# Which products in parts of the array stand together: whole sets of scores, and values behind the next scores

## The chip, the cores and the metric

The kernel runs on one core of a Trainium2 chip. The metric is the device time of one execution in microseconds (us). An execution with the hardware profiler attached gives the trace; its own time stands beside the times of the runs without it.

## The reference

One step of a hybrid encoder layer, for 512 frames of a prompt and for 8 samples with 16 new frames each (640 tokens of width 1024, all float32). Cut to what matters:

```
x += 0.5 * SwiGLU_1(norm(x))                  # width 2816
h  = norm(x);  z = h @ w_in_mix               # one projection for both mixers and the gates
x += (g_ret * Br_ret(retention) + g_fox * Br_fox(fox)) @ w_out
x += 0.5 * SwiGLU_2(norm(x))
x += (p @ W_ple) * sigmoid(norm(x) @ W_ple_gate)

fox, prompt : 8 heads of 64; causal softmax(q k^T / 8 + c_i - c_j) v, in blocks of 128 queries
fox, sample : 16 queries against 1024 cached keys and values and 16 new ones, per sample and head
retention   : 4 heads, key width 128, value width 256; 512 prompt frames in chunks, and per
              sample one chunk of 16 on a given state; the new states are outputs
```

The new keys, values, forget values and retention states are outputs too.

## The kernel before

The work is written as one long program, and a planner (the framework's scheduler, with a timeline of its own) puts each engine's instructions in an order; among what is ready by that timeline it takes what stands earlier in the program. On the chip each engine then runs its own list in that order.

Stages: the first SwiGLU; then, from about 470 to 1020 us of the span, the mixer; then the output projections, the second SwiGLU and the embedding. In the mixer a stream of *units* (`run_units`, line 845: projections of 256 columns, their weights split in two parts for exactness) is the bulk of TensorE's work. `fill(us)` (line 1582) writes so many us of units into the program, and between two fills the steps of the attention and of the retention are written: sixteen sets of the prompt's attention (lines 1604 to 1611), eight samples of eight steps (1617 to 1621), four heads of retention (1641 to 1651). `defer(us, f)` (line 760) writes `f` later, when the program's estimated clock has moved on by so much; `pump` writes what is due. `after(inst, name, why)` (line 209) orders one instruction behind another in the planner's list; on the chip it is no wait. `load` (line 212) issues from SyncE's queue.

TensorE's array has 128 rows and 128 columns. A product with 64 rows of weights or fewer, or 64 columns or fewer, takes a part of the array, and several stand side by side in it. Four kinds of them are touched here; each float32 product shows as two weight loads and two products in the trace (the pick products as one):

- *Prompt scores* (`prompt_scores`, line 1164): for head pair `pr` and query block `i` two heads in 64 rows each, one bank a head: first a product that brings the bias (`pick`, 40 rows), then queries times keys.
- *Prompt values* (`values`, line 1202): two heads in 64 columns each, for `i + 1` key blocks, into one bank; written by `defer(1.5, ...)` after the second head's weights have been flipped and copied.
- *Sample scores and values* (`Sample`, line 1221): four pairs of heads in 32 columns each. A sample has two halves (`s`) of 512 cached frames: a half's scores are four products of 512 columns, written 1.8 us after the copy of the fourth pair's transposed keys. The values are 36 products of 128 columns, written in three parts, each after the flip of its part of the weights (`flip`, line 1298).
- *Retention, samples* (`values_s`, line 1419, four lanes of 32 columns; `states`, line 1464, four lanes of 32 rows into four banks).

In the order of the lanes the kernel before always begins with the first, and the `after` lines tie the first lane behind the work that the others need:

```
if r == 0:
    for _, made in four[2:]:
        after(m, made.ins.name, "the four pairs of heads side by side in the array")
```

Buffers that this touches: six banks of the tag `pa`, eight tiles of the tag `att` (transposed keys, softmax weights, flipped weights), and four buffers of 1 MB (`kv`) in which two halves of keys and two of values pass. `Sample.loads` (line 1233) writes the loads in the order: next keys' first half, both halves of values, next keys' second half.

Of the kernel before, what the change touches and what calls it, by code (L numbers as in the profile page):

```python
# [19 lines left out]
P = 128  # L20
# [111 lines left out]
def kernel(  # L132
# [1028 lines left out]

    pair_bank, pair_pts = [None], [None, None]

    def prompt_scores(hu, pr, i):

        n, both = (i + 1) * P, pair()
        for h2, ps in enumerate(both):
            head, rows = hu * 4 + 2 * pr + h2, slice(h2 * FD, h2 * FD + 40)
            last = mm(ps[:, :n], pick[rows, head:head + 1].to_broadcast([40, P]), c_row[0][rows, :n], True, False, skip_group_check=True)
        for h2, ps in enumerate(both):  # L1170
            rows = slice(h2 * FD, (h2 + 1) * FD)
            m = mm(ps[:, :n], qk_out[hu][rows, 0, pr, i * P:n], qk_out[hu][rows, 1, pr, :n], False, True, skip_group_check=True)
            if h2 == 0:
                after(m, last.ins.name, "the pair of heads side by side in the array")
        for h2, ps in enumerate(both):
            prompt_softmax(hu, 2 * pr + h2, i, n, ps)

    def prompt_softmax(hu, h, i, n, ps):
# [12 lines left out]
        def flipped():  # L1191
            pt = bank()
            for j in range(i + 1):
                transpose(pt[:, j * P:(j + 1) * P], pe[:, j * P:(j + 1) * P])
            pts = att()
            done = nc.scalar.copy(pts[:, :n], pt[:, :n])
            pair_pts[h % 2] = (pts, done)
            if h % 2 == 1:
                both = list(pair_pts)
                defer(1.5, lambda: values(both))  # L1200

        def values(both):
            pr = h // 2
# [3 lines left out]
            for j in range(i + 1):  # L1207
                for h2 in range(2):
                    m = mm(po[h2 * FD:(h2 + 1) * FD, i * P:n], v_p[hu][j][:, (2 * pr + h2) * FD:(2 * pr + h2 + 1) * FD],
                           both[h2][0][:, j * P:(j + 1) * P], j == 0, j == i, skip_group_check=True)  # L1210
                    if j == 0 and h2 == 0:
                        after(m, both[1][1].ins.name, "the pair of heads side by side in the array")
            if i == 3:
# [7 lines left out]
    class Sample:  # L1221
# [20 lines left out]
        def step(self, n):  # L1242
# [15 lines left out]
            kts = att()  # L1258
            if pr % 2 == 0:
                done = nc.vector.tensor_copy(kts, pt)  # L1260
            else:
                done = nc.scalar.copy(kts, pt)
# [4 lines left out]
            if pr == 3:  # L1267
                four = self.kts

                def scores():  # L1270

                    for r, (kt, _) in enumerate(four):
                        m = mm(self.ps[s][r * 32:(r + 1) * 32, :], qof(r, self.b), kt, False, True, skip_group_check=True)
                        if r == 0:
                            for _, made in four[2:]:
                                after(m, made.ins.name, "the four pairs of heads side by side in the array")
                    nc.vector.tensor_reduce(self.mx[:, s:s + 1], self.ps[s], axis=AX.X, op=ALU.max)
                    if s == 1:
                        self.softmax()
# [18 lines left out]
        def flip(self, s):  # L1298
            if s == 0:
                nc.vector.tensor_reduce(self.rc, self.sums, axis=AX.X, op=ALU.add)  # L1300
                nc.vector.reciprocal(self.rc, self.rc)
                self.po = bank()
            n = 4 if s < 2 else 1
# [6 lines left out]
            else:  # L1310
                nc.scalar.copy(pts[:, :n * P], pt[:, :n * P])
            defer(1.5, lambda: self.values(s, pts, n))

        def values(self, s, pts, n):
            for j in range(n):
                for pr in range(4):
                    rhs = (self.v[4 * s + j] if s < 2 else vnew)[:, pr * P:(pr + 1) * P]
                    mm(self.po[pr * 32:(pr + 1) * 32, :P], pts[:, j * P + pr * 32:j * P + (pr + 1) * 32], rhs,
                       s == 0 and j == 0, s == 2, skip_group_check=True)
            if s == 2:  # L1320
                om = tmp([P, P])
                nc.vector.scalar_tensor_tensor(om, self.po[:, :P], self.rc, cs["bd"], op0=ALU.mult, op1=ALU.mult)
                defer(1.5, lambda: self.fold(om))

# [8 lines left out]
    class Retention:  # L1333
# [130 lines left out]
        def states(self):  # L1464
# [3 lines left out]
            for j in range(2):  # L1468
                for r in range(NB // 2):
                    rows = slice(r * 32, (r + 1) * 32)  # L1470
# [133 lines left out]
    for hu in (0, 1):  # L1604
# [3 lines left out]
        for pr in range(2):  # L1608
            for i in range(4):
                prompt_scores(hu, pr, i)  # L1610
                fill(2 * (FILL_P0 if hu == 0 else FILL_P1))
    samples = [Sample(b) for b in range(NB)]
    defer(0.0, sample_new)
# [27 lines left out]
    for hd, r in enumerate(heads):  # L1641
        for step in (
            lambda: r.rotate(0), lambda: r.rotate(1), lambda: (r.flip(), heads[hd + 1].first_loads() if hd + 1 < RH else None),
            lambda: r.scores(), lambda: r.scores_s(),
            lambda: (r.states_p(), heads[hd + 1].loads() if hd + 1 < RH else None),
            lambda: r.values(0), lambda: r.values(1), lambda: r.values_s(),
            lambda: (r.sizes(), until(("rg", hd)), r.gates()),
            lambda: (r.states(), heads[hd + 1].more_loads() if hd + 1 < RH else None), lambda: r.finish(),
        ):
# [131 lines left out]
```

## Time and profile before

| | |
|---|---|
| median of three runs | 1638.36 us (1637.53 to 1638.69) |
| the profiled execution | 1636.49 us, span 1634.5 us |
| TensorE busy | 1624.8 us, 11979 products |
| VectorE, ScalarE, GpSimd busy | 1164.5, 733.1, 94.5 us |
| memory traffic | 242.88 MB, mean 149 GB/s |
| a 1 MB load of cached values, issue to landing | 6.7 us (median) |
| a 1 MB load of cached keys, issue to landing | 6.2 us (median) |

How to read the rows: PE is TensorE's product, PEld its weight load (in the trace both have an entry), DVE VectorE, ACT ScalarE, POOL GpSimd, SPq SyncE's queue. L205 is a line of the kernel; many products have the line of the helper `mm`, so they are told apart by the tiles (`pa<-kv,att`: written and read) and by their form: `128*32` is a weight load of 128 rows and 32 columns. In brackets stands how long the engine was idle before and what ended that; "issue" is no other engine.

### The profile page before, as it was taken

How to read it: one execution, taken by the hardware profiler on the slowest of the kernel's cores; microseconds unless marked ns; L12 is line 12 of the kernel's file. 1: busy time of each engine (PE TensorE's matmuls, PEld its weight loads, DVE VectorE, ACT ScalarE, POOL GpSimd, SP SyncE). 2: the span in 40 equal slices, each digit the busy share in tenths (PEclk: the TensorE clock that was granted, in tenths of full speed). 3: DMA queues.
4: the chain of work that ended last, by engine and by line, in shares of the span. 5: the costliest groups of instructions: out<-in, count | busy, mean ns of one | idle time of the engine just before them, and what ended most of it. 6: DMA issues, size and time to landing. Idle time of an engine off the chain costs nothing.

```text
span 1634.5 us, 30303 instructions
## 1 busy us (share of the span) xinstructions
PE 1624.8 (99%) x11979; PEld 1555.4 (95%) x11979; DVE 1164.5 (71%) x2472; ACT 733.1 (45%) x1536; POOL 94.5 (6%) x172
## 2 busy tenths in 40 slices
PE   9999999999999999999999999999999999999999
PEld 8999999999999888888789898999999999999998
DVE  7985786577776755767688996557885787578663
ACT  7552354244455444444334454435553355235432
POOL 0000000000011111000000011001000000000000
PEclk9999999999999999999999999999999999999999
DMA  7244233433533234566776477534334323332531
GB/s 247 78 144 142 86 94 118 150 94 108 186 107 104 99 113 138 210 254 249 284 248 209 159 258 261 177 101 163 98 100 142 126 82 132 135 118 88 173 122 46
DMA packets 205566, 242.88 MB, mean 149 GB/s; under 512 B 10176, under 2 KB 175984, under 8 KB 201328
## 3 DMA queue, kind: packets, MB, share of 16 engines
q1 hardware_dynamic: 193824, 200.07, 37.0%
q0 software_dynamic: 11392, 40.79, 6.3%
q8 instruction: 94, 1.54, 0.4%
q14 instruction: 48, 0.39, 0.1%
q10 hardware_dynamic: 208, 0.08, 0.0%
HBM read 194.89 MB, written 46.03 MB: 147 GB/s over the span
## 4 chain that ended last, share of the span: by engine, by line
PE 97%; ACT 1%; DVE 1%; DMA 1%; issue 0%; SPq 0%; DVEq 0%
PE pa L205 74%; PE pg L205 19%; PE pa L228 4%; ACT tmp L533 0%; DMA raw<-in_ffn_w_in_dram 0%; PE pg L228 0%; ACT wh L282 0%; DMA kv<-in_x_prompt_dram 0%; DVE kv L1474 0%; ACT blk L361 0%; DVE wl L283 0%; DVE raw L424 0%; DVE tmp L573 0%; ACT blk L353 0%; DVE raw L420 0%
## 5 line engine op out<-in xcount | busy, mean ns | idle before, releaser
L282 ACT CAST wh<-raw 128x512 fp32r<-128x512 f32 (+1 forms) x525 | 315.8, 613 | 493.2 <-PE pa L205 315.0
L205 PE MATMUL pa<-blk,wh 128*128 128x320 f32 x2344 | 509.0, 310 | 1.9 <-ACT wh L282 0.9
L283 DVE TENSOR_TENSOR wl<-raw,wh 128x512 fp32r<-128x512 f32 (+1 forms) x525 | 352.0, 679 | 95.2 <-ACT wh L282 91.5
L205 PEld LDWEIGHTS pa<-blk,wh 128*128 128x128 f32 x2344 | 386.8, 188 | 8.5 <-ACT wh L282 2.3
L205 PE MATMUL pa<-blk,wl 128*128 128x320 f32 x1172 | 343.0, 309 | 0.0
L205 PE MATMUL pa<-kv,wh 128*128 128x320 f32 x1344 | 251.6, 308 | 0.0
L205 PEld LDWEIGHTS pa<-blk,wl 128*128 128x128 f32 x1172 | 215.4, 188 | 0.1
L205 PEld LDWEIGHTS pa<-kv,wh 128*128 128x128 f32 x1344 | 210.7, 188 | 0.0
L205 PE MATMUL pg<-blk,wh 128*128 128x320 f32 x768 | 176.6, 316 | 1.1 <-DVE blk L833 1.1
L205 PE MATMUL pa<-blk,blk 128*128 128x320 f32 (+2 forms) x1064 | 168.7, 304 | 0.0
L205 PE MATMUL pa<-kv,wl 128*128 128x320 f32 x672 | 154.6, 308 | 0.0
L205 PEld LDWEIGHTS pa<-blk,blk 128*128 128x128 f32 (+1 forms) x1064 | 151.8, 183 | 2.0 <-PE pa L205 1.2
L205 PE MATMUL pg<-wh,blk 128*128 128x256 f32 x768 | 148.4, 286 | 0.0
L205 PEld LDWEIGHTS pg<-blk,wh 128*128 128x128 f32 x768 | 127.4, 188 | 8.0 <-issue 4.1
L205 PEld LDWEIGHTS pg<-wh,blk 128*128 128x128 f32 x768 | 120.8, 188 | 6.4 <-issue 5.2
L205 PE MATMUL pg<-blk,wl 128*128 128x320 f32 x384 | 118.8, 309 | 0.0
L205 PEld LDWEIGHTS pa<-kv,wl 128*128 128x128 f32 x672 | 112.6, 188 | 0.0
L205 PE MATMUL pg<-wl,blk 128*128 128x256 f32 x384 | 108.4, 283 | 0.0
L205 PE MATMUL pa<-wh,blk 128*128 128x256 f32 (+1 forms) x432 | 82.3, 285 | 0.0
L283 DVE TENSOR_TENSOR blk<-raw,blk 128x512 fp32r<-128x512 f32 x82 | 56.3, 689 | 34.8 <-ACT blk L282 23.6
L282 ACT CAST blk<-raw 128x512 fp32r<-128x512 f32 x82 | 50.6, 621 | 51.8 <-DMA raw<-in_ffn_w_in_dram 41.5
L205 PEld LDWEIGHTS pg<-wl,blk 128*128 128x128 f32 x384 | 72.2, 188 | 1.6 <-issue 1.1
(287 smaller groups left out, 2225.4 us busy)
## 6 DMA issues: line engine op xcount, KB each, us to landing
raw<-in_ffn_w_in_dram SPq DMA_DIRECT2D x86, 512.0 KB, 4.7
raw<-in_w_in_mix_dram SPq DMA_DIRECT2D x25, 1024.0 KB, 5.6
raw<-in_ffn_w_out_dram SPq DMA_DIRECT2D x16, 1024.0 KB, 5.1
kv<-in_cache_fox_k_dram SPq DMA_DIRECT2D x16, 1024.0 KB, 6.2
kv<-in_cache_fox_v_dram SPq DMA_DIRECT2D x16, 1024.0 KB, 6.7
blk<-xd SPq DMA_DIRECT2D x48, 320.0 KB, 5.4
xd<-blk POOLq DMA_DIRECT2D x40, 320.0 KB, 3.0
zdram<-blk POOLq DMA_DIRECT2D x24, 320.0 KB, 4.0
```

Source lines behind the costliest of these rows:

```text
L205: i = nc.tensor.matmul(out, lhsT, rhs, start=start, stop=stop, **kw)
L228: tick(nc.tensor.transpose(out, in_, ident[: in_.shape[0], : in_.shape[0]]), 0.11)
L282: nc.scalar.copy(hi, src)
L283: nc.vector.tensor_tensor(lo, src, hi, op=ALU.subtract)
```

## The change

1. Prompt scores: the lanes run second head first, for the bias and for the scores; the `after` hangs on the second head's score.
2. Prompt values: no longer written by `defer(1.5, ...)`. They go into a list `values_due`, and the next set of scores, of the prompt or of a sample, writes them directly behind its last product, with an `after` on it. The second head goes first, behind the first head's copy. What is left after the prompt is written 7 us later.
3. Sample scores: fourth pair first, ordered behind the copies of the other three. The copies of pairs 0 and 1 are on VectorE and those of 2 and 3 on ScalarE (before: 0 and 2, 1 and 3).
4. Sample values: the three parts are collected, and all 36 products are written in one run behind the next sample's first scores (the last sample's 1.5 us after its last flip). Their bank is taken then.
5. Retention: `states` loops over its four banks from the last, and is written in the same step as `values_s`, two steps earlier than before; the next head's state load stays in its step.

```diff
--- before.py
+++ after.py
@@ -1159,19 +1159,21 @@
         nc.vector.tensor_reduce(mnew, snew, axis=AX.X, op=ALU.max)
 
 
-    pair_bank, pair_pts = [None], [None, None]
+    pair_bank, pair_pts, values_due = [None], [None, None], []
 
     def prompt_scores(hu, pr, i):
 
         n, both = (i + 1) * P, pair()
-        for h2, ps in enumerate(both):
+        for h2, ps in ((1, both[1]), (0, both[0])):
             head, rows = hu * 4 + 2 * pr + h2, slice(h2 * FD, h2 * FD + 40)
             last = mm(ps[:, :n], pick[rows, head:head + 1].to_broadcast([40, P]), c_row[0][rows, :n], True, False, skip_group_check=True)
-        for h2, ps in enumerate(both):
+        for h2, ps in ((1, both[1]), (0, both[0])):
             rows = slice(h2 * FD, (h2 + 1) * FD)
             m = mm(ps[:, :n], qk_out[hu][rows, 0, pr, i * P:n], qk_out[hu][rows, 1, pr, :n], False, True, skip_group_check=True)
-            if h2 == 0:
+            if h2 == 1:
                 after(m, last.ins.name, "the pair of heads side by side in the array")
+        while values_due:
+            values_due.pop(0)(m)
         for h2, ps in enumerate(both):
             prompt_softmax(hu, 2 * pr + h2, i, n, ps)
 
@@ -1197,19 +1199,21 @@
             pair_pts[h % 2] = (pts, done)
             if h % 2 == 1:
                 both = list(pair_pts)
-                defer(1.5, lambda: values(both))
-
-        def values(both):
+                values_due.append(lambda behind: values(both, behind))
+
+        def values(both, behind):
             pr = h // 2
             if i == 0:
                 pair_bank[0] = bank()
             po = pair_bank[0]
             for j in range(i + 1):
-                for h2 in range(2):
+                for h2 in (1, 0):
                     m = mm(po[h2 * FD:(h2 + 1) * FD, i * P:n], v_p[hu][j][:, (2 * pr + h2) * FD:(2 * pr + h2 + 1) * FD],
                            both[h2][0][:, j * P:(j + 1) * P], j == 0, j == i, skip_group_check=True)
-                    if j == 0 and h2 == 0:
-                        after(m, both[1][1].ins.name, "the pair of heads side by side in the array")
+                    if j == 0 and h2 == 1:
+                        after(m, both[0][1].ins.name, "the pair of heads side by side in the array")
+                        if behind is not None:
+                            after(m, behind.ins.name, "with the other products in parts of the array")
             if i == 3:
                 f = blk([P, S])
                 nc.vector.tensor_copy(f, po)
@@ -1256,7 +1260,7 @@
             for j in range(4):
                 transpose(pt[:, j * P:(j + 1) * P], self.k[4 * s + j][:, pr * P:(pr + 1) * P])
             kts = att()
-            if pr % 2 == 0:
+            if pr < 2:
                 done = nc.vector.tensor_copy(kts, pt)
             else:
                 done = nc.scalar.copy(kts, pt)
@@ -1269,11 +1273,14 @@
 
                 def scores():
 
-                    for r, (kt, _) in enumerate(four):
+                    for r in (3, 2, 1, 0):
+                        kt = four[r][0]
                         m = mm(self.ps[s][r * 32:(r + 1) * 32, :], qof(r, self.b), kt, False, True, skip_group_check=True)
-                        if r == 0:
-                            for _, made in four[2:]:
+                        if r == 3:
+                            for _, made in four[:3]:
                                 after(m, made.ins.name, "the four pairs of heads side by side in the array")
+                    while values_due:
+                        values_due.pop(0)(m)
                     nc.vector.tensor_reduce(self.mx[:, s:s + 1], self.ps[s], axis=AX.X, op=ALU.max)
                     if s == 1:
                         self.softmax()
@@ -1299,7 +1306,7 @@
             if s == 0:
                 nc.vector.tensor_reduce(self.rc, self.sums, axis=AX.X, op=ALU.add)
                 nc.vector.reciprocal(self.rc, self.rc)
-                self.po = bank()
+                self.pts = []
             n = 4 if s < 2 else 1
             pt = bank()
             for j in range(n):
@@ -1309,18 +1316,24 @@
                 nc.vector.tensor_copy(pts[:, :n * P], pt[:, :n * P])
             else:
                 nc.scalar.copy(pts[:, :n * P], pt[:, :n * P])
-            defer(1.5, lambda: self.values(s, pts, n))
-
-        def values(self, s, pts, n):
-            for j in range(n):
+            self.pts += [pts[:, j * P:(j + 1) * P] for j in range(n)]
+            if s == 2:
+                if self.b + 1 < NB:
+                    values_due.append(self.values)
+                else:
+                    defer(1.5, lambda: self.values(None))
+
+        def values(self, behind):
+            po = bank()
+            for j, pt in enumerate(self.pts):
                 for pr in range(4):
-                    rhs = (self.v[4 * s + j] if s < 2 else vnew)[:, pr * P:(pr + 1) * P]
-                    mm(self.po[pr * 32:(pr + 1) * 32, :P], pts[:, j * P + pr * 32:j * P + (pr + 1) * 32], rhs,
-                       s == 0 and j == 0, s == 2, skip_group_check=True)
-            if s == 2:
-                om = tmp([P, P])
-                nc.vector.scalar_tensor_tensor(om, self.po[:, :P], self.rc, cs["bd"], op0=ALU.mult, op1=ALU.mult)
-                defer(1.5, lambda: self.fold(om))
+                    rhs = (self.v[j] if j < 8 else vnew)[:, pr * P:(pr + 1) * P]
+                    m = mm(po[pr * 32:(pr + 1) * 32, :P], pt[:, pr * 32:(pr + 1) * 32], rhs, j == 0, j == 8, skip_group_check=True)
+                    if j == 0 and pr == 0 and behind is not None:
+                        after(m, behind.ins.name, "with the other products in parts of the array")
+            om = tmp([P, P])
+            nc.vector.scalar_tensor_tensor(om, po[:, :P], self.rc, cs["bd"], op0=ALU.mult, op1=ALU.mult)
+            defer(1.5, lambda: self.fold(om))
 
         def fold(self, om):
             pf = bank()
@@ -1466,7 +1479,7 @@
             hd = self.hd
             pss = [bank() for _ in range(NB // 2)]
             for j in range(2):
-                for r in range(NB // 2):
+                for r in reversed(range(NB // 2)):
                     rows = slice(r * 32, (r + 1) * 32)
                     mm(pss[r][:, j * DV:(j + 1) * DV], self.kb[rows, j, :], self.vs[4][rows, :], True, True)
             for r in range(NB // 2):
@@ -1609,6 +1622,7 @@
             for i in range(4):
                 prompt_scores(hu, pr, i)
                 fill(2 * (FILL_P0 if hu == 0 else FILL_P1))
+    defer(7.0, lambda: [values_due.pop(0)(None) for _ in range(len(values_due))])
     samples = [Sample(b) for b in range(NB)]
     defer(0.0, sample_new)
     samples[0].load(samples[0].k, cache_k)
@@ -1643,9 +1657,9 @@
             lambda: r.rotate(0), lambda: r.rotate(1), lambda: (r.flip(), heads[hd + 1].first_loads() if hd + 1 < RH else None),
             lambda: r.scores(), lambda: r.scores_s(),
             lambda: (r.states_p(), heads[hd + 1].loads() if hd + 1 < RH else None),
-            lambda: r.values(0), lambda: r.values(1), lambda: r.values_s(),
+            lambda: r.values(0), lambda: r.values(1), lambda: (r.values_s(), r.states()),
             lambda: (r.sizes(), until(("rg", hd)), r.gates()),
-            lambda: (r.states(), heads[hd + 1].more_loads() if hd + 1 < RH else None), lambda: r.finish(),
+            lambda: heads[hd + 1].more_loads() if hd + 1 < RH else None, lambda: r.finish(),
         ):
             step()
             fill(FILL_R)
```

## Rows read from the trace of the kernel before

**Rows 1.** The page: busy time of the engines, and the chain that ended last

```profile
PE 1624.8 (99%) x11979; PEld 1555.4 (95%) x11979; DVE 1164.5 (71%) x2472; ACT 733.1 (45%) x1536; POOL 94.5 (6%) x172
...
PE 97%; ACT 1%; DVE 1%; DMA 1%; issue 0%; SPq 0%; DVEq 0%
```

**Rows 2.** Waits of TensorE's products, 500 to 1030 us: who for whom, total, times, longest

```profile
PE pg L205 <- DVE blk L833: 1.1, 1, 1.1
PE pa L228 <- DVE att L1188: 0.3, 1, 0.3
```

**Rows 3.** Waits of the weight loads, 500 to 1030 us

```profile
PEld pa L205 <- issue: 15.5, 70, 0.8
PEld pa L228 <- issue: 11.6, 29, 0.8
```

**Rows 4.** Timeline of the weight loads, prompt values: start, us, engine, count

```profile
639.85 0.31 PEld L205 LDWEIGHTS pg<-wh,blk 128*128 128x128 f32 x2
640.29 0.19 PEld L205 LDWEIGHTS pa<-att,kv 128*64 128x64 f32 x2
640.65 0.19 PEld L205 LDWEIGHTS pg<-wl,blk 128*128 128x128 f32 x1 [0.17 <-issue]
...
641.08 0.85 PEld L205 LDWEIGHTS pa<-att,kv 128*64 128x64 f32 x14
642.10 0.19 PEld L205 LDWEIGHTS pg<-wh,blk 128*128 128x128 f32 x1 [0.17 <-issue]
```

**Rows 5.** The same timeline, prompt values with scores, and a set of scores alone

```profile
585.33 0.85 PEld L205 LDWEIGHTS pa<-att,kv 128*64 128x64 f32 x14
...
586.87 0.19 PEld L205 LDWEIGHTS pg<-wh,blk 128*128 128x128 f32 x1
...
620.96 0.19 PEld L205 LDWEIGHTS pa<-att,pick 40*128 40x128 f32 x2
...
621.98 0.19 PEld L205 LDWEIGHTS pg<-wh,blk 128*128 128x128 f32 x1 [0.54 <-issue]
```

**Rows 6.** The same timeline, sample scores and values in three stretches of time

```profile
688.00 0.16 PEld L205 LDWEIGHTS pa<-blk,tmp 128*32 128x32 f32 x8 [0.15 <-issue]
688.36 0.19 PEld L205 LDWEIGHTS pg<-blk,wl 128*128 128x128 f32 x1 [0.20 <-issue]
688.70 0.16 PEld L205 LDWEIGHTS pa<-att,blk 128*32 128x32 f32 x8 [0.15 <-issue]
689.70 0.30 PEld L205 LDWEIGHTS pa<-sm,tmp 128*128 128x128 f32 x2 [0.84 <-DVE tmp L1322]
...
719.05 0.14 PEld L205 LDWEIGHTS pa<-att,blk 128*32 128x32 f32 x4 [0.19 <-issue]
720.03 0.42 PEld L228 LDWEIGHTS pa<-sm,kv 128*128 128x128 f32 x4 [0.84 <-DVE blk L827]
...
802.60 0.81 PEld L205 LDWEIGHTS pa<-kv,att 128*32 128x32 f32 x32
...
804.68 0.19 PEld L205 LDWEIGHTS pa<-blk,blk 128*128 128x128 f32 x1 [0.20 <-PE pa L205]
```

**Rows 7.** Groups by line and form on VectorE, 650 to 850 us: the keys' copies

```profile
L1260 DVE COPY att<-pa 128x512 f32<-128x512 f32 x31 | 21.3, 688 | 7.7 <-PE pa L228 7.4
```

**Rows 8.** Timeline of SyncE's queue: a pair of value loads

```profile
709.83 1.60 SPq L214 DMA_DIRECT2D kv<-in_cache_fox_v_dram  x2
```

**Rows 9.** Timeline of the weight loads, retention: state products

```profile
925.38 0.31 PEld L205 LDWEIGHTS pa<-kv,tmp 32*128 32x128 f32 x8 [0.19 <-PE pa L205]
926.02 0.30 PEld L205 LDWEIGHTS pg<-blk,wh 128*128 128x128 f32 x2 [0.33 <-issue]
926.28 0.19 PEld L205 LDWEIGHTS pg<-blk,wl 128*128 128x128 f32 x1
```

**Rows 10.** Busy time by stage: PE, PEld, DVE, ACT, POOL, clock, DMA

```profile
650.00:840.00 190.00, 189.99 (x1683) 157.76 (x1681) 129.91 (x277) 81.58 (x183) 13.98 (x23) 1.00 0.67 245
840.00:960.00 120.00, 118.88 (x868) 110.70 (x867) 112.39 (x242) 51.50 (x114) 9.06 (x15) 1.00 0.58 199
```

## The prediction

> **What bounds the kernel now.** I read the page first: TensorE is busy for 99% of the span, and the chain that ended last lies on it for 97% [rows 1]. So the end is set by how long TensorE's own stream lasts. Then I read the waits in the attention and retention (500 to 1030 us): TensorE's products waited for another engine for 1.4 us in all [rows 2]. The same view for the weight loads tells something else: 27.1 us of idle in 99 places ahead of its loads for one kind of bank, put down to "issue", that is, to no other engine [rows 3]. The timeline shows what these are [rows 4]. Whole-array loads come 0.117 us apart; the second of the pair at 639.85 starts at 639.97, so the next was due at 640.08. It comes at 640.29, because it is the first for half of the array's columns; and it is 640.65 before a whole-array load comes again. Two loads for a part of the array cost 0.20 + 0.36 = 0.56 us of the stream. The fourteen left over from the same set cost 0.20 + (642.10 - 641.08) = 1.22 us, for what a whole set of sixteen at 615.23 also takes. What goes ahead alone is paid in full. I call such an unbroken run of part-array products a stretch, and its cost the time from the last whole-array load ahead of it to the first behind it, less one pitch. That is the currency of this change.
>
> Added up over the timeline: the prompt's attention has 39 stretches of 39.1 us together (first at 513.78, last at 641.08), the samples' 40 of 52.0 us (655.87 to 843.36), the retention 18 of 19.0 us (864.26 to 1007.57). PE time alone is at stake, 110 us of it.
>
> **The change part by part.** The number of products stays. What changes is in how many stretches they stand.
>
> *Prompt scores.* A whole set costs 1.22 us for three key blocks [rows 5], and 0.27 more or less a block: 0.69, 0.95, 1.22, 1.49 us, together 4.35, four times. Before, five of the sixteen sets are broken, either because the first head's pick product goes ahead while the second head's bank is still taken, or because one head's scores go alone. The new order begins with the head whose bank comes last, so that the other is ready when it starts.
>
> *Prompt values.* A set costs 0.57, 0.79, 1.00, 1.22 us for one to four blocks, 3.58 together, four times. Six of sixteen are broken like the one above: the first head's product waits only until the second head's copy has been placed, not until it is done. The new order starts with the head that is copied last. Both kinds whole and apart: 4 x (4.35 + 3.58) = 31.7 us. Now the values also stand directly behind scores. Such a joint is there once before: fourteen value loads with a one-block set cost 0.20 + (586.87 - 585.33) = 1.74 us [rows 5], apart 1.22 + 0.69 = 1.91. A joint of two splits, rows then columns, saves 0.17; fifteen save 2.5. With 1.1 us for the samples' new-frame scores, which stay: 30.3. **Saved: 39.1 - 30.3 = 8.8 us.**
>
> *Samples.* A whole set of scores (eight loads) costs 0.20 + (689.70 - 688.70) = 1.20 us, and half a set, four loads, 0.20 + (720.03 - 719.05) = 1.18 [rows 6]: four lanes run in the time of two. Nine of sixteen sets stand in two pieces and two more are interleaved lane by lane with values, since the copies of the last pairs of keys (0.69 us on VectorE [rows 7]) end after the first lane has started. The change starts with the last pair. The 36 value products of a sample come in three runs of 32, 32 and 8 loads, mostly apart; eight alone cost 0.19 + (688.36 - 688.00) = 0.55 us. Behind scores they pay no entry of their own, since both split columns in four: forty value loads and eight score loads stand together once, for 0.20 + (804.68 - 802.60) = 2.28 us [rows 6], so a value load adds (2.28 - 1.20) / 40 = 0.027. Seventy-two with the scores: 2.28 + 32 x 0.027 = 3.14. Seven samples at 3.14 + 1.20, the first one's 2 x 1.20, the last one's values alone 0.55 + 64 x 0.027 = 2.28: 35.1 us. **Saved: 52.0 - 35.1 = 16.9 us.**
>
> Here a rule speaks against the change, and a row answers it. The row: eight loads of a column-split set are through in 0.16 us [rows 6]. The Trainium skill, "TensorE: Matmul & The Clock Gate", section "Part 3: Packing small matmuls", says that a weight load overlaps running products only where its row group differs. All lanes of the samples' scores and values read rows 0 to 127; by that rule whole sets would gain nothing, some 10 of the 16.9 us would not come, and the sum below would end near 1624. The trace disagrees with it at these shapes, so I keep the 16.9.
>
> *What the samples' move drags along.* Values now run after the next sample's first scores, so the two value buffers, two transposed blocks and a bank are given back then. The value loads stand in SyncE's queue ahead of later key and weight loads. Before, the pair at 709.83 [rows 8] is issued right as values and next scores pass (708.7 to 711.9); afterwards at the same place or up to 3 us later. Landing takes 6.7 us (the profile's table), and these values are multiplied from 731.5 on: 13 us of cover; a key or weight load behind them has at least as long. The bank is now taken for 3 us instead of some ten. The later multiply, fold and store have no reader before the branch projection. The swapped copies leave 16 a sample-half on either engine: nothing.
>
> *Retention.* The state products (16 loads, rows split in four) move two steps up, behind the samples' values. With them move four VectorE updates (0.68 us each) ahead of the root and scaling, and a store on GpSimd's queue; the next state's load stays where it was. Eight loads cost 0.20 + (926.02 - 925.38) = 0.84 us [rows 9]; a second eight adds 0.43 (twelve, at 972.07, cost 1.28), so a whole set 1.27. Before, they stand in two to four pieces a head, their banks coming free one by one; the reversed order waits for the last bank. Values cost 1.23 whole, but in three heads one lane goes ahead for 0.95, and nothing in the diff ends that; I keep it. One place where columns then rows join saves 0.24. So 4 x (1.23 + 1.27 - 0.24) + 3 x 0.95 = 11.9. **Saved: 19.0 - 11.9 = 7.1 us.**
>
> *Taken off.* Behind a stretch the stream makes up 0.03 us (two loads in 0.26 us [rows 9], where the usual pitch of these makes 0.29): 97 stretches become about 43, so 1.6. From 840 to 960 us VectorE is busy 112.4 of 120 us [rows 10] (the same rows show the clock granted in full), and TensorE cannot run far ahead of what it prepares; I take half of the retention's gain away, 3.5 (bounds 0 and 7.1). Sets will still be cut where an earlier matrix product becomes ready between two lanes; before, about one in ten is cut without its own operand being late. Four more pieces at 0.8: 3.2 (bounds 0 and 12).
>
> Sum: 8.8 + 16.9 + 7.1 - 1.6 - 3.5 - 3.2 = 24.5 us. The profiled execution took 1636.5, so 1612.0; the median of the runs is 1.9 us above it, so **1614**. What bounds it afterwards is the same stream. Without the last two discounts it is 1607; with the upper ends of both, 1626.
>
> **Rivals.** *The sets stay in pieces.* The order on TensorE is made by the planner by its own times, and products from earlier in the program go first. For it: sets are cut now although all their operands are there (values of the retention, scores at 513.78 to 518.03). Against it: most prompt sets after 560 us, with the old order, are already whole. If half of the gain goes this way: 1638.4 - 12 = 1626.
>
> *The wait for the last operand moves onto TensorE (slower).* Each set now begins with its latest operand. The planner's times are not the chip's; where it takes a copy to be done that is not, TensorE stands, in order, with everything behind it. Price: up to one copy, 0.69 us [rows 7], in each of about 64 sets: 44 us, which gives 1638 - 24 + 44 = 1658. It decides from a mean of 24/64 = 0.38 us a set. Against it: before, after the same kind of copies, such waits sum to a few us in 500 us [rows 2, 3], at similar distances.
>
> *VectorE becomes the bound.* With 16 us less of TensorE from 650 to 840, VectorE's 129.9 in 190 us [rows 10] become 75%; only 840 to 960 has no room. If all that the retention and the last two samples gain is given back there: 1638 - 24 + 7 = 1621, inside the range.
>
> **How the numbers follow.** Forecast 0.70 (its own range 1607 to 1624), sets in pieces 0.15, the rule on column splits 0.01, VectorE 0.04 on top of what is taken off, the wait for the last operand 0.07, and 0.03 for pieces and waits that cancel. A measurement of this kernel tells about 0.2% (3.3 us) from no change. Faster 0.88, same 0.05, slower 0.07. The range 1605 to 1631 leaves out the slower case and the worst of the pieces.
>
> **What would show it.** Right: between 500 and 1030 us the weight loads' "issue" idle falls from the 99 places of [rows 3] to under 60; score loads come in eights with 72 value loads in the same stretch; state loads stand in sixteens; TensorE's busy share stays 99%. Wrong: score loads in fours and sixes; new waits of the first load of a set for a copy or a bank; TensorE idle for VectorE after 840 us; value loads landing behind their use.

## The result, and the profile after

Time after: 1622.67 us median of 5 runs (1621.34 to 1622.75), against 1638.36 us (1637.53 to 1638.73): ratio 0.9903, 95% interval 0.9888 to 0.9917. The kernel is 15.7 us faster; 24.4 were forecast (1614), and the time lies inside the range of 1605 to 1631. The profiled execution took 1622.67 us; that of before was 1.9 us under its median, so the two profiles are 13.8 us apart.

The page after shows the same bound as [rows 1]:

```profile
PE 1609.3 (99%) x11979; PEld 1557.3 (96%) x11979; DVE 1164.4 (72%) x2472; ACT 731.5 (45%) x1536; POOL 94.5 (6%) x172
...
PE 96%; DMA 2%; DVE 1%; ACT 1%; issue 0%; SPq 0%; DVEq 0%
```

The weight loads' waits from 500 to 1030 us answer [rows 3]. Columns: who for whom, total us, times, longest.

```profile
PEld pa L205 <- issue: 14.0, 57, 0.8
PEld pa L228 <- issue: 8.7, 16, 0.8
```

The 99 places have become 73, where under 60 were expected. Added up over the timeline in the prediction's own currency, the stretches became:

| part | before: count, us | forecast whole, us | after: count, us |
|---|---|---|---|
| prompt | 39, 39.1 | 30.3 | 35, 36.3 |
| samples | 40, 52.0 | 35.1 | 18, 35.8 |
| retention | 18, 19.0 | 11.9 | 15, 18.0 |
| sum | 97, 110.1 | 77.3 | 68, 90.1 |

So 20.0 us of stretches went, 16.2 of them from the samples. The timeline of the weight loads shows the samples as they were forecast, in place of [rows 6]: eight score loads, 64 of the values and 8 of the new frame's values, until a whole-array load comes again.

```profile
683.08 0.16 PEld L205 LDWEIGHTS pa<-att,blk 128*32 128x32 f32 x8 [0.19 <-issue]
683.54 0.13 PEld L205 LDWEIGHTS pa<-kv,att 128*32 128x32 f32 x4 [0.30 <-issue]
683.97 1.66 PEld L205 LDWEIGHTS pa<-kv,att 128*32 128x32 f32 x60 [0.30 <-issue]
685.60 0.24 PEld L205 LDWEIGHTS pa<-blk,tmp 128*32 128x32 f32 x8
686.04 0.42 PEld L228 LDWEIGHTS pa<-sm,kv 128*128 128x128 f32 x4 [0.20 <-PE pa L205]
```

Entry, loads and exit take 0.19 + (686.04 - 683.08) = 3.15 us; 3.14 was forecast. Six such runs stand in the trace, where seven were forecast: one sample's 72 value loads (786.62 us) stand apart from the scores, for 2.30 us. All sixteen sets of scores come in eights; those that stand alone cost 1.19 to 1.23 us.

The prompt and the retention look otherwise. The same timeline, in order: the prompt's first sets, still lane by lane as before; a single pick product ahead of its set; and, in the retention, two state loads that join the values, the other fourteen 4 us later (compare [rows 9]).

```profile
525.38 0.29 PEld L205 LDWEIGHTS pa<-kv 64*128 64x128 f32 x2
526.01 0.19 PEld L205 LDWEIGHTS pg<-wh,blk 128*128 128x128 f32 x1 [0.33 <-ACT att L1037]
...
613.57 0.18 PEld L205 LDWEIGHTS pa<-att,pick 40*128 40x128 f32 x1
613.88 0.19 PEld L205 LDWEIGHTS pg<-wh,blk 128*128 128x128 f32 x1
614.19 0.18 PEld L205 LDWEIGHTS pa<-att,pick 40*128 40x128 f32 x1
614.20 0.41 PEld L205 LDWEIGHTS pa<-kv 64*128 64x128 f32 x4
...
907.82 0.29 PEld L205 LDWEIGHTS pa<-kv,tmp 32*128 32x128 f32 x2 [0.41 <-issue]
...
912.16 0.74 PEld L205 LDWEIGHTS pa<-kv,tmp 32*128 32x128 f32 x14 [0.20 <-PE pg L205]
```

New is a wait of TensorE at the change from samples to retention. TensorE's products there; the last number is the idle time ahead of the row:

```profile
828.86 0.31 PE L205 MATMUL pg<-blk,wl 128*128 128x320 f32 x1
831.75 0.57 PE L205 MATMUL pa<-sm,tmp 128*128 128x64 f32 x2 [2.59 <-DVE tmp L1335]
...
833.04 0.73 PE L205 MATMUL pa<-blk,wh 128*128 128x320 f32 x2
833.57 0.47 PE L205 MATMUL pa<-blk,wl 128*128 128x320 f32 x1
833.84 0.73 PE L205 MATMUL pa<-blk,wh 128*128 128x320 f32 x2
...
835.39 0.46 PE L205 MATMUL pg<-blk,wh 128*128 128x320 f32 x2
835.69 0.31 PE L205 MATMUL pg<-blk,wl 128*128 128x320 f32 x1
835.83 0.46 PE L205 MATMUL pg<-blk,wh 128*128 128x320 f32 x2
```

Behind the wait three products take 833.84 - 833.04 = 0.80 us, from 835.39 on 0.44: the granted clock is at its half level, 1.2 GHz, from 831.9 to 835.3. The twelve products from 832.09 to 835.39 take 3.30 us where 12 x 0.147 = 1.76 would do: 1.5 us. VectorE's timeline shows who is waited for:

```profile
825.19 0.69 DVE L424 TENSOR_TENSOR raw<-raw 128x512 f32<-128x512 f32 x1
829.88 1.56 DVE L1374 TENSOR_TENSOR kv<-kv,blk 128x640 f32<-128x640 f32 x2 [4.00 <-DMA blk<-in_c_rope_dram]
831.36 0.34 DVE L1335 SCALAR_TENSOR_TENSOR tmp<-pa,ty,sm 128x128 f32<-128x128 f32 x1
```

The last sample's masked sums (L1335) stand in VectorE's queue behind the retention's first rotation (L1374), and this one waits 4.00 us for the rope tables, which SyncE issues here:

```profile
813.95 4.23 SPq L214 DMA_DIRECT2D kv<-zdram  x6
...
822.05 1.16 SPq L214 DMA_DIRECT2D blk<-in_c_rope_dram  x2
```

Before, the first table was issued at 830.86 us and the rotation (line 1361 there) began at 840.30:

```profile
830.86 0.43 SPq L214 DMA_DIRECT2D blk<-in_c_rope_dram  x1
...
840.30 0.82 DVE L1361 TENSOR_TENSOR kv<-kv,blk 128x640 f32<-128x640 f32 x1
```

After, the two are 7.8 us apart, and for 4.0 of them VectorE stands ready. The last sample's scores run 20 us earlier (811.9 instead of 832 us), the tables are issued only 9 us earlier.

### The profile page after: what moved, and what is told of

The parts are those of the page before. It is cut to its first block, busy times and chain, and to the rows that moved or that the text cites. A ratio compares the mean times of both kernels' runs of the same rounds, so it can differ in the third digit from the quotient of the medians.

```text
span 1620.9 us, 30289 instructions
## 1 busy us (share of the span) xinstructions
PE 1609.3 (99%) x11979; PEld 1557.3 (96%) x11979; DVE 1164.4 (72%) x2472; ACT 731.5 (45%) x1536; POOL 94.5 (6%) x172
## 4 chain that ended last, share of the span: by engine, by line
PE 96%; DMA 2%; DVE 1%; ACT 1%; issue 0%; SPq 0%; DVEq 0%
PE pa L205 74%; PE pg L205 18%; PE pa L228 4%; DMA kv<-zdram 1%; DMA blk<-in_c_rope_dram 0%; DMA raw<-in_ffn_w_in_dram 0%; ACT tmp L533 0%; PE pg L228 0%; DVE wl L283 0%; ACT wh L282 0%; DMA kv<-in_x_prompt_dram 0%; SPq L214 0%; DVE kv L1487 0%; ACT blk L361 0%; DVE blk L1473 0%
```

## The experiments

The runs of the kernel before beside these had medians of 1637.86 (17 runs), 1637.89 (15) and 1638.09 us (7).

**The three parts by themselves.** Each kernel is the one before with one part of the diff: `s_alone` the samples, `p_alone` the prompt, `r_alone` the retention. `s_order` has the samples' new order of lanes and copies alone, the values staying in three runs:

```diff
-            if pr % 2 == 0:
+            if pr < 2:
...
-                    for r, (kt, _) in enumerate(four):
+                    for r in (3, 2, 1, 0):
+                        kt = four[r][0]
...
-                        if r == 0:
-                            for _, made in four[2:]:
+                        if r == 3:
+                            for _, made in four[:3]:
```

> The samples' part of the change alone (lanes in reverse, copies swapped, 36 values in one run behind the next scores), prompt and retention as before. Theory (what is saved is the time of the stretches): the samples' stretches fall from 40 with 51.9 us to 18 with about 35, so 17 us less; 2.8 us come back where TensorE waits for the last sample's masked sums and 1.7 us where its clock is halved after that wait, if that wait is there in this kernel too: 1622 to 1625 us. Rival (the stretches cost less than they look, and the gain of the whole change comes from all three parts): 1628 to 1633.

Measured 1626.76 us (1626.01 to 1627.04), ratio 0.9931 (0.9915 to 0.9948): 11 us. That is between the two expectations, 1.8 us over the theory's range and 1.2 under the rival's.

> Of the samples' part only the order of the lanes and the swapped copies; values in three parts as before. Theory: eleven broken sets of scores become whole, each worth 1.0 to 1.2 us less what is already joined: 9 to 11 us less, 1627 to 1630 us, so that the run of 36 values is worth the other 6 us of the samples' part. Rival (the copies end as late as before and the sets wait for them in the array's own queue): 1635 to 1640.

Measured 1627.08 us (1626.17 to 1627.27), ratio 0.9933 (0.9918 to 0.9948), as expected: the order of the lanes, with the copies that were swapped for it, gives nearly all that the whole samples' part gives. What was expected besides, that the run of 36 values is worth the other 6 us, did not come (see below).

> The prompt's part alone. Theory: only the six broken value sets are mended (six times 0.56 us); the joints fail since the values' own copies are not done when the next scores run, and single bias products still go ahead: about 2.6 us less, 1635 to 1637 us. Rival (the prediction's 8.8 us are there, and the whole change loses them again elsewhere): 1629 to 1631.

Measured 1633.08 us (1632.43 to 1634.60), ratio 0.9972 (0.9961 to 0.9982): 4.8 us, between the two expectations. Its stretches from 500 to 1030 us add up to 106.2 us, 3.9 less than before: 2.8 in the prompt, and 1.1 in the samples, which this edit doesn't touch.

> The retention's part alone (state products from the last bank and two steps earlier). Theory: banks are given out as they come free, whichever lane asks first, so the reversed order mends little: 18 stretches become 14, 1 to 2.5 us less, 1636 to 1637.5 us. Rival (VectorE is the bound from 840 to 960 us, and four updates ahead of the scaling make it worse): 1639 to 1642.

Measured 1637.03 us (1636.67 to 1638.66), ratio 0.9996 (0.9986 to 1.0005): inside the theory's range and outside the rival's, but a gain cannot be told from none. The stretches did fall, as the theory had it, from 18 to 14 in the retention, by 1.2 us. Against that TensorE waits 3.8 us between 500 and 1030 us, where it waited 1.4 before [rows 2]. The two longest waits are new; they end at 992.84 and 1010.45 us:

```profile
PE pa L205 <- DVE att L1401: 1.3, 1, 1.3
PE pg L205 <- DVE blk L1537: 1.1, 1, 1.1
```

The gains of the three parts add up to 11.1 + 4.8 + 0.8 = 16.7 us, where the whole change gives 15.7.

Why does the run of 72 value loads add nothing to the order alone? Its stretches are there: `s_order` has 99.9 us from 500 to 1030, `s_alone` 93.8; 4.5 of the 6.1 us lie in the samples, 1.7 in the retention. The waits of TensorE's products in this stretch, first of `s_alone`, then of `s_order`:

```profile
PE pa L205 <- DVE tmp L1331: 2.1, 1, 2.1
```

```profile
PE pa L228 <- DMA tmp<-in_p_prompt_dram: 0.8, 1, 0.8
```

L1331 of `s_alone` are the masked sums; `s_order` has no wait of over 0.3 us but the one shown. The windows from 828 to 840 us (busy us of PE, PEld, DVE, ACT, POOL, granted clock, DMA share, GB/s), again first of `s_alone`:

```profile
828.00:840.00 12.00, 9.89 (x61) 9.62 (x58) 8.48 (x16) 2.81 (x5) 0.97 (x2) 0.86 0.88 312
```

```profile
828.00:840.00 12.00, 12.00 (x137) 10.88 (x136) 11.14 (x21) 4.00 (x9) 0.10 (x1) 1.00 1.05 375
```

So the longer run is paid back at the change to the retention, by the wait (2.1 us) and the half clock behind it (about 1.5); some 2.5 of the 6.1 us I can't place.

The order also decides on the rule that spoke against the change. The Trainium skill, "TensorE: Matmul & The Clock Gate", section "Part 3: Packing small matmuls", has a weight load overlap only where its row group differs. By that sentence, taken alone, lanes that all read rows 0 to 127 would run one after another. Here a whole set costs 1.20 us and half a set 1.18 [rows 6], and `s_order`, which changes only the lanes' order and the copies that go with it, gains 10.8 us. If the lanes ran one after another, joining two halves would save no more than one entry and exit, 0.38 us by `lone` below, in each of the eleven broken sets: some 4 us, an estimate. That is not the nothing of which the prediction speaks, but less than half of what came. The measurements decide against the rule for this shape.

**The wait at the change.** `om_first` puts the rotation behind the masked sums, an order on VectorE alone:

```diff
-            nc.vector.tensor_tensor(r, r, tab[0], op=ALU.mult)
+            i = nc.vector.tensor_tensor(r, r, tab[0], op=ALU.mult)
+            if self.hd == 0:
+                after(i, samples[NB - 1].om.ins.name, "the last sample goes first")
```

> The changed kernel, with one order added on VectorE: the first rotation of the retention (L1374 of the changed kernel, which waits 4.00 us there for its rope tables) goes behind the last sample's masked sums (L1335). Theory (the wait of 2.6 us for those sums before the last sample's fold, and the 3.4 us at half clock after it, are what the changed kernel gives back at the change from the samples to the retention): both go, 2.6 + 1.7 = 4.3 us, 1617.5 to 1619.5 us. Rival (the retention has nothing else ready, TensorE then waits the same time for the rope tables one step on): 1621.5 to 1623 us, with a wait of over 1.5 us on VectorE's rotated keys between 830 and 850 us. Second rival (the wait goes, the clock stays as it was): 1620 us.

Measured 1623.06 us (1621.38 to 1623.13), ratio 0.9905 (0.9889 to 0.9920). The theory fell. Of the first rival the main point held, the wait has moved, though to another name than the rotated keys. TensorE's products:

```profile
830.65 0.31 PE L205 MATMUL pa<-blk,wl 128*128 128x320 f32 x1
833.33 0.56 PE L205 MATMUL pg<-blk,wh 128*128 128x320 f32 x2 [2.37 <-DVE blk L830]
```

L830 makes the next projection's operand, and on VectorE it stands behind the rotation, which still waits for the tables. `early_om` therefore leaves this order and brings the tables in earlier:

```diff
     for b in range(NB):
+        if b == 7:
+            tab = []
+            for n in range(2):
+                r = blk()
+                load(r, c_rope[n])
+                tab.append(r)
...
-    tab = []
-    for n in range(2):
-        r = blk()
-        load(r, c_rope[n])
-        tab.append(r)
```

Both multiplications by the tables are kept behind the last masked sums; `om_first` tied only the first.

> om_first, with the two rope tables loaded ahead of the last sample's steps (two blocks are held some 20 us longer); VectorE's order stays that of om_first. It asks whether the wait of 2.4 to 2.9 us at the change from samples to retention, which only moved in om_first, comes from the late rope tables. Theory (it does, and the 3.4 us at half clock follow from the wait): no wait over 1 us of TensorE between 820 and 850 us, the clock full there, 1617.5 to 1619.5 us. Rival (the next late load takes their place, the rotated key and value rows from zdram, issued at 813.95 us and landing 8 us later, or the retention's state and masks): a wait of over 1.5 us between 825 and 850 us on another name, 1621 to 1623 us. Second rival (the wait goes, but the clock falls as before): 1620 us.

Measured 1619.97 us (1618.66 to 1622.48), ratio 0.9887 (0.9871 to 0.9904). VectorE no longer waits, and the masked sums run 5 us earlier:

```profile
826.26 0.34 DVE L1335 SCALAR_TENSOR_TENSOR tmp<-pa,ty,sm 128x128 f32<-128x128 f32 x1
826.52 3.02 DVE L1374 TENSOR_TENSOR kv<-kv,blk 128x640 f32<-128x640 f32 x4
```

The clock is full from 828 to 840 us (1.00, where `om_first` had 0.86). What is late next is VectorE's own work, and once ScalarE's, in three shorter waits of TensorE between 836 and 845 us:

```profile
PE pg L205 <- DVE blk L836: 1.2, 1, 1.2
...
PE pa L205 <- DVE wl L283: 0.6, 1, 0.6
PE pg L205 <- ACT tmp L820: 0.5, 1, 0.5
```

So the late tables were the cause of the long wait, and the half clock went with it. But of the 4.1 us of both, 2.2 come back in the three shorter waits. One of them, of 1.2 us, is longer than the 1 us that the theory allowed, and the median is 0.5 us above its range. It equals the time of the second rival, which the full clock rules out. By the medians this is the fastest kernel here, 2.7 us under the changed one; the intervals of the two ratios overlap.

**The prompt's joints.** `seen` writes a head's values behind a set of scores only if they were already due one set earlier:

```diff
-        while values_due:
+        for _ in range(seen[0]):
             values_due.pop(0)(m)
+        seen[0] = len(values_due)
```

> The changed kernel, but a prompt head's values are put behind a set of scores only if they were already due at the scores before, so that their own copies are done by then. Theory (the joints of the prompt, of which the prediction counted 15 and the changed kernel shows 3, are missed because the copies of the transposed scores on ScalarE and VectorE are not done when the next scores run): eight stretches less, each about 0.40 us, 3 us: 1619 to 1620.5 us, and the sum of the prompt's stretches falls from 36.3 to about 33 us. Rival (a joint saves only the one pitch of a load, 0.17 us, as the prediction took it): 1.4 us, 1621 to 1621.7 us. Second rival (values one step later hold up the banks of the next heads): 1623 us or more.

Measured 1623.56 us (1622.29 to 1624.51), ratio 0.9911 (0.9897 to 0.9924). The stretches fell as in the first rival: eight fewer, and 36.3 became 35.0 us, 0.16 each. The joint is there, 16 value loads right behind a set of scores:

```profile
565.13 0.37 PEld L205 LDWEIGHTS pa<-kv 64*128 64x128 f32 x4
566.04 0.85 PEld L205 LDWEIGHTS pa<-att,kv 128*64 128x64 f32 x16 [0.54 <-issue]
```

The time didn't follow. It is the second rival's, but that banks are held up no row shows. The waits of TensorE, 500 to 1030 us, add up to 5.6 us, where the changed kernel has 3.2, and hold two that it hasn't, beside the one for the masked sums (2.1):

```profile
PE pa L228 <- DVE tmp L1052: 1.2, 1, 1.2
...
PE pg L205 <- DVE blk L833: 0.9, 1, 0.9
```

**All orders at once.** `new_rp` has those of `om_first` and `seen`, and puts the first lane of the prompt's single picks and of the retention's values behind the newest whole-array product written ahead:

```diff
+        if rhs.dtype == F32R and lhsT.shape[0] == P:
+            newest[0] = i.ins.name
...
+            if h2 == 1:
+                after(last, ahead, "behind what is written ahead of it")
...
+                    if j == 0 and pr == 0:
+                        after(m, newest[0], "behind what is written ahead of it")
```

> The changed kernel with three orders added: the one of om_first, the one of seen, and the first lanes of the prompt's single picks and of the retention's values_s put behind the newest whole-array product that was written ahead of them. Theory (stretches are cut because products that were written earlier and become ready in between go first, and each cut costs about 0.40 us, entry and exit together): 14 stretches less than in the changed kernel, 5.6 us, and 4.3 us at the change to the retention: 1613 to 1615 us. Rival (the products in part of the array now wait for the whole-array ones ahead of them, and their readers come late): 1616 to 1619 us, with new waits of TensorE on pa or pg between 500 and 1000 us. Second rival (only the number of products, not of stretches, sets the cost): 1618 us, as om_first.

Measured 1629.33 us (1626.42 to 1632.52), ratio 0.9947 (0.9934 to 0.9959): slower than the changed kernel by 6.7 us. Against `seen` the prompt's stretches did become 24 instead of 27, and 32.6 us instead of 35.0. The 2.4 us are those of the first three sets of scores, which are whole now (0.9 for two, 1.0 for the third), and of one single pick (0.5); five single picks still go ahead. It was the rival that happened, and harder than it was priced. TensorE's longest waits:

```profile
PE pa L230 <- DVE att L1457: 3.6, 1, 3.6
PE pg L205 <- DVE blk L832: 2.5, 1, 2.5
PE pa L230 <- DVE tmp L1054: 1.8, 1, 1.8
PE pg L205 <- DVE blk L1560: 1.6, 1, 1.6
```

Three of them (3.6, 2.5 and 1.6 us) are followed by the half clock, as the windows show (columns as above):

```profile
830.00:840.00 10.00, 7.84 (x46) 7.80 (x47) 10.00 (x18) 1.00 (x3) 1.86 (x3) 0.83 0.65 217
980.00:990.00 10.00, 8.44 (x50) 7.51 (x46) 5.37 (x9) 6.82 (x17) 0.00 (x0) 0.83 0.58 197
1008.00:1018.00 10.00, 6.33 (x32) 5.62 (x31) 6.64 (x25) 0.62 (x1) 1.99 (x3) 0.83 0.37 148
```

Against the changed kernel that is 3.2 us less in stretches, 7.0 more in waits (10.2 instead of 3.2), and two more half clocks at about 1.5 us: 6.8 us longer by this estimate, 6.7 by the medians.

**The price of a stretch.** `lone` adds one product of 16 columns ahead of each group of transposes:

```diff
+            nc.tensor.matmul(pt[:32, :16], qof(0, self.b), self.k[4 * s][:, pr * P:pr * P + 16], start=True, stop=True, skip_group_check=True)
             for j in range(4):
                 transpose(pt[:, j * P:(j + 1) * P], self.k[4 * s + j][:, pr * P:(pr + 1) * P])
```

> The changed kernel, with one product of 16 columns in a quarter of the array's columns added before the transposes of each sample step (64 of them; what they write is written over by the transposes, so nothing reads it). They stand alone between whole-array products: 54 stretches more. It is the price of a stretch by itself. Theory (a stretch costs about 0.40 us to enter and leave, whatever is in it): 54 x 0.40 = 22 us and the products' own work of 64 x 0.03 us: 1642 to 1649 us. Rival (only the work in it counts, the sums of the stretches are those of their loads and columns): 64 x 0.05 = 3 us at most: 1623 to 1626 us.

Each shows as two products on the chip. Measured 1639.22 us (1637.43 to 1639.90), ratio 1.0006 (0.9997 to 1.0015): the 54 small stretches cost 16.6 us and with them all that the change gains. One of them in the timeline:

```profile
665.88 0.19 PEld L205 LDWEIGHTS pa<-blk,wl 128*128 128x128 f32 x1
666.26 0.14 PEld L1260 LDWEIGHTS pa<-kv,blk 128*32 128x32 f32 x2 [0.20 <-issue]
666.43 0.14 PEld L228 LDWEIGHTS pa<-sm,kv 128*128 128x128 f32 x1
```

666.43 - 665.88 less the pitch of 0.147 is 0.40 us; over all stretches, (110.8 - 90.1) / 54 = 0.38. The theory's price held. The time came out under its 1642 to 1649, since TensorE now reaches the change to the retention later: the wait there is 1.4 instead of 2.6 us, and the clock stays full. 54 x 0.38 = 20.7 us, less 1.2 for the wait, 1.5 for the clock and the prediction's make-up of 54 x 0.03 = 1.6, is 16.4. The Trainium skill, "TensorEngine Tiling (Array Packing)", section "Key Properties", says that a change of the tiling mode, unlike one of the tile, drains TensorE. The trace agrees in that the way in and out costs time, 0.38 us for both together; that it goes into a drain, no row here shows.

## Why the prediction was right, and where it was not

The currency was right. TensorE's stream is the end, whole stretches in place of pieces shorten it, and that a small stretch costs what it does because of its entry and exit, `lone` shows by itself.

*Samples: right.* 16.9 us were forecast, 16.2 came, in the form that was forecast: sets in eights at 1.20, runs of 80 loads at 3.15.

*Prompt: 8.8 forecast, 2.8 came.* The six broken value sets are mended, as forecast. The step that failed is "The new order begins with the head whose bank comes last, so that the other is ready when it starts". Seven score sets are still in pieces; by the same count there were six before, where the prediction has five, a number that its sum doesn't use. Against whole ones at 0.69 to 1.49 they cost 0.9 (the two sets of 514.66 to 525.38), 1.0 (530.78), 0.5 (550.35), 0.6 (572.01), 0.3 (605.94) and 0.5 us (613.57): 3.8 together. Reversing the lanes doesn't help there. In the last four a single pick product goes ahead; as I read it, a bank goes to whichever lane asks first, so that again the first has one and the second none, but no run shows the banks. In the other three, half of the 3.8 us, both heads' pick products stand together and a head's scores go alone, the other way of breaking that the prediction names. `new_rp`, which holds the first pick product back, makes these three whole. Second, of "fifteen" joints behind scores two came (566.09 and 583.30), since the values' own copies (L1198 on ScalarE, L1190 on VectorE) weren't done when the next scores ran, which `seen` bears out: put one set later, eleven of the joints are there. That is 13 x 0.17 = 2.2 us. Their size was right (0.16 in `seen`), their number wasn't.

*Retention: 7.1 forecast with 3.5 taken off, 1.0 came.* The same failed assumption: "the reversed order waits for the last bank". The states still stand in pieces of 4, 4, 6 and 2 (first head), 2 and 14, 2 and 14, 6, 2 and 8; `r_alone` shows no gain that can be measured. More than half of the shortfall was in the discount, for another reason (VectorE).

*Taken off: 8.3 us, from the planned 32.8 of stretches.* Of the 32.8 only 20.0 came, so 12.8 were lost in stretches where 3.5 + 3.2 had been set aside. That the time still lies in the range is in part luck: the discounts, meant for VectorE and for sets cut by other products, paid for joints that failed and a wait that nobody had foreseen. From 20.0 to the 13.8 of the two profiles another 6.2 us went:

- the wait at the change, 2.6, and the half clock behind it, 1.5. No step of the prediction has them: "What bounds it afterwards is the same stream" didn't ask what the earlier end of the samples runs into. `early_om` shows the late tables to be the cause. The 1.5 belongs to the profiled execution: over the five the mean granted clock was 0.998, 1.000, 0.998, 0.999 and 0.999, and the one at 1.000 took 1622.72 us, no less than the others. What the half clock adds to the median stays open;
- 0.9 ahead of the attention, where both kernels have the same instructions (first prompt scores at 514.66 instead of 513.78);
- the 1.4 us of [rows 2] are gone, 0.6 came elsewhere (L1473 and L830): 0.8 back;
- 0.03 for each of the 29 stretches less, 0.9, as the prediction's make-up;
- which leaves 6.2 - 4.1 - 0.9 + 0.8 - 0.9 = 1.1 us that I can't place.

*The rivals.* Sets staying in pieces happened in the prompt and the retention, not in the samples; at 1626 it was priced from half of the gain, and 64% came in the medians. The wait for the last operand didn't come: no set waits for a copy on TensorE's products. In `new_rp`, which forces the order further, waits did cost more than the stretches gave, but of transposes and whole-array products, not of a set's first load. VectorE as the bound decided between 840 and 960 us neither here (0.4 us of waits) nor in `r_alone` (1.1 us, as before); behind 960 us the two waits above, 2.4 us, outweigh the 1.2 us that the stretches of `r_alone`'s profiled execution give, and in `early_om` it is what is late next.

## What to carry to other kernels

Small products that use a part of the array cost by the stretch, here 0.38 us to get in and out and 0.17 us saved where two kinds join, so count stretches before products. Put the lane whose operand is copied last first, which with the swapped copies is worth 10.8 us in the samples; in the prompt's scores and in the retention, where the last bank was to decide the order, it mended little. And when a stage ends 20 us earlier, look up the loads of the next stage: if their issue is tied to buffers and to a queue, they need not move as far (9 us here), and the wait can be paid twice, once as itself and once in the clock.

## What the runs showed of the hardware

After or in waits of TensorE of 2.6 (changed kernel), 2.1 (`s_alone`, `seen`), 2.4 (`om_first`), 2.5 and 3.6 us (`new_rp`) the granted clock fell to its half level and stood there for 3.4 us, also after one of 1.6 us (`new_rp`, from 980.49 us), but not after 1.8 us (`new_rp`, from 535.2 us) or 1.4 us (`lone`): length alone doesn't decide it in these rows. In the profiled execution the wait of 2.6 us so costs about 4.

At the start of the kernel, executions differ likewise with the same instructions. Eight products (L256, first at 6.46 us) take 2.08 us in the profile of `s_order`, where the full level is first granted at 9.8 us; in that of the changed kernel, where it is granted from 5.9 us on, they take 1.16. The clock then falls again for 3.4 us from 12.7 us on in the changed kernel's profile and for 6.8 from 10.8 on in that of `early_om`, in that of `s_order` not at all. The first prompt scores start between 513.78 (before) and 515.51 us (`p_alone`): 1.7 us that belong to no edit.
